# Starting the value sums with their first real products, and moving a row scaling from GpSimd to VectorE, in a transformer layer on one core

## The chip, the cores and the metric

The kernel runs on one core of one Trainium2 chip. The metric is device time of one execution in microseconds; lower is better. One program, written by hand for the five engines of the core, does the whole layer: TensorE multiplies, VectorE (DVE in the profile), ScalarE (ACT) and GpSimd (POOL) do elementwise work, and SyncE (SP) issues nearly all DMAs. Every engine takes its instructions strictly in the order in which the program lists them for it; one that has to wait holds those behind it.

## The reference

One layer over 2048 tokens of width 1024, with a context of 256 tokens, in float32. Cut to what matters here:

```
h  = modulate(rmsnorm(x), sh1, sc1)                 # and the same for the context
rq, rk, rv, rg, aq, ak, av = split(h @ w_in)
ret = gated bidirectional retention over rq, rk, rv  # 4 heads of 128, chunks of 128 tokens
q, k = rope(rmsnorm(aq)), rope(rmsnorm(ak))          # 8 heads of 64, 2 key/value heads
p   = softmax(q k^T / 8)                             # over 2304 keys (context and tokens)
att = p @ v
x  = x + g1 * (concat(ret, att) @ w_out)
h2 = modulate(rmsnorm(x), sh2, sc2)
x  = x + g2 * (relu(h2 @ w_ff1)^2 @ w_ff2)
out = rmsnorm(x)
```

The two places that the change touches are the sums `p @ v`, and the row scaling inside the second `rmsnorm(x)`, that of `h2`.

## The kernel before

**Precision.** Most products are made of parts: a float32 operand is split into a hi part (float16) and a lo part (what hi leaves out), and hi x hi, hi x lo and lo x hi are summed in PSUM.

**Stages.** The first stage (0 to about 690 us) computes the projections. The second (691 to about 1640) is attention, with the retention, the output projection and the second norm of finished token tiles woven in. The third (from about 1690) is the MLP. A scheduler orders the first stage; from attention on the order is written out by hand. There, work is entered with `on(k, phase, fn)` under a step number k and one of 13 phases; the steps run in order, and within each the phases: `begin, scores, piece, maximum, early, exp, cast, low, chain, pe, values, late, dma`. What is entered first in a phase of a step runs first. After the phases maximum, low and late, one link of a chain of small operations is also run (`link`); `settle(what)` runs links until the one wanted has been issued.

**Attention.** There are 32 groups (16 tiles of 128 queries, from the last tile to the first, times 2 key heads); a group has 18 steps, one for each tile of 128 keys. In every step TensorE makes the scores of one key tile (lines 202 and 203) and one piece of the products whose maximum the next group needs (line 165); VectorE reduces the piece (line 178); ScalarE takes the exponential (208) and, for two key tiles at once, the hi part (212); the lo part is made on GpSimd (219) for five of the nine pairs of key tiles and on VectorE (221) for the other four. `Group.values(j)` then multiplies the pair j: for each key tile and each of four heads, lo times the first 65 columns of the values, and hi times all 129 (values, a column of ones for the sum of p, and the values' lo part). Two heads share one PSUM bank, so a group has two banks `o`. Before the first pair, each bank is set by one product of a tile of zeros with 258 columns of values (`start=True`); everything after adds to it. Line 227 is that product, 235 and 236 are the lo and hi products. ScalarE evacuates the banks at the end of the group (240, 241).

**Output tiles.** For each token tile, `output_tile(t, k, last)` enters: the transposes of the retention half and of the attention half (line 1259, in steps k-11 and k-6), their hi parts on ScalarE and lo parts (`rl`, `al`) on VectorE (line 1266, steps k-9 and k-4), 16 x 3 products with w_out (1274 to 1276), the residual's additions on VectorE (1281), the squares' sums on ScalarE (1288), the store of the new x to DRAM on SP's queue (1291), and the chain for the root: a sum on VectorE (1295) and two operations on GpSimd (1009, and the power at 1010, `cy_f`). `made` is the step of the second addition; the store and the root are entered in step made+1, and `norm` in phase late of step made+4: it multiplies the whole tile `xr` (128 x 1024, in place) by the root, on GpSimd (1301). The transposes of the result (1306), their modulation on VectorE (1311) and GpSimd (1316) and their store follow some steps later. Tiles are 35 steps apart. For the last but one tile (t=1) made is step 619, so its norm is entered in step 623; for the last one (t=0) made is 642 and its norm is in step 646, and its transposes are taken up inside the MLP's first block.

**The start of the MLP.** The `prelude` (from step 606 on) enters loads and the forms of the first-layer weights (1451 on GpSimd, 1460 on ScalarE, 1461 on VectorE) and the first four of seven up products (1522 to 1524), whose sums are formed on VectorE (1545). After the last step the loop over the MLP's blocks begins; its first block holds up products 4 to 6 with their sums, the relu (1533, ScalarE), the squares (1534, GpSimd), the split of u (70, ScalarE; 71, VectorE), the split of the second-layer weights (70, 71), and then the down products (1582 to 1584) with the addition to the accumulator on VectorE (1585).

Of the kernel before, what the change touches and what calls it, by code (L numbers as in the profile page):

```python
# [13 lines left out]
F16 = mybir.dt.float16  # L14
# [3 lines left out]
ALU = mybir.AluOpType  # L18
# [4 lines left out]
P = 128  # L23
# [16 lines left out]
VW = 2 * HD + 1  # L40
# [14 lines left out]
def layer_kernel(ctx: ExitStack, tc: tile.TileContext, a: dict, out: bass.AP):  # L55
    nc = tc.nc
    mm = nc.tensor.matmul
# [76 lines left out]
    wv = kp.tile([P, 2, NK, VW + 1], F16, name="wv")  # L134
# [6 lines left out]
    class Group:  # L141
# [81 lines left out]
        def values(self, j):  # L223
            if j == 0:
                self.o = [psV.tile([P, 2, VW], F32, name=f"o{b}", tag=f"o{b}") for b in range(2)]
                for o in self.o:
                    mm(o, zeros, wv[:, 0, :2, :VW], start=True, stop=False)
            hi, lo = self.hi.pop(j), self.lo.pop(j)
            for i in range(2):
                v = wv[:, self.g, 2 * j + i]  # L230
                for h in range(4):
                    o = self.o[h // 2][:, h % 2]
                    c = slice(h * P, (h + 1) * P)
                    last = 2 * j + i == NK - 1 and h % 2 == 1
                    mm(o[:, : HD + 1], lo[:, i, c], v[:, : HD + 1], start=False, stop=False)  # L235
                    mm(o, hi[:, i, c], v[:, :VW], start=False, stop=last)  # L236

        def evacuate(self):
            self.so = op.tile([P, 4, VW], F32, name="so", tag="so")
# [20 lines left out]
    with ExitStack() as st:  # L260
# [630 lines left out]
        for n, (g, c) in enumerate(todo):  # L891
# [7 lines left out]
            last = c == len(PLAN[g]) - 1  # L899
# [49 lines left out]
    def pool(stack, name, bufs=1, **kw):  # L949
        return stack.enter_context(tc.tile_pool(name=name, bufs=bufs, reuse_waits="tile", **kw))  # L950
# [3 lines left out]
    vp = pool(attn, "vp")  # L954
# [12 lines left out]
    nc.vector.tensor_tensor(unit, ident[:, 64:65], ident[:, 96:97], op=ALU.add)  # L967
    nc.vector.tensor_tensor(unit, unit, ident[:, 80:81], op=ALU.add)
    nc.vector.tensor_scalar_mul(unit, unit, ROW)
    zeros = vp.tile([P, P], F16, name="zeros")  # L970
    nc.vector.memset(zeros, 0.0)
    mts = [vp.tile([P, 4, P], F32, name=f"mt{i}") for i in range(2)]
    for mt in mts:
        nc.gpsimd.memset(mt, 0.0)
# [27 lines left out]
    def settle(what):  # L1002
        while what not in settled:
            link()
# [243 lines left out]
    def output_tile(t, k, last):  # L1248
        y = {}
# [48 lines left out]

        def norm():
            settle(("f", t))  # L1300
            nc.gpsimd.tensor_scalar(y["x"], y["x"], y["r"], 1.0, op0=ALU.mult, op1=ALU.mult)

        def transpose_x(q):
            y["ps"] = bank(1)
# [33 lines left out]
        on(made + 1, "dma", store_x)  # L1338
        on(made + 1, "late", root)
        on(made + 4, "late", norm)  # L1340
        if last:
            for q in range(2):
# [53 lines left out]
    for n, t in enumerate(range(NT - 1, -1, -1)):  # L1396
        made_at, last = output_tile(t, R0 + 43 + RF * n, n == NT - 1)
# [410 lines left out]
```

## Time and profile before

| | |
|---|---|
| median of 3 runs | 2942.72 us (2941.49 to 2947.78) |
| the profiled execution | 2946.76 us |
| its span, first to last instruction | 2945.0 us |
| mean granted TensorE clock | 0.987 |
| HBM read, written | 272.52 MB, 71.46 MB |

| stretch, us | what runs | PE busy | DVE busy | ACT busy | POOL busy |
|---|---|---|---|---|---|
| 0 to 691 | projections | 629.05 | 476.70 | 233.07 | 287.58 |
| 691 to 1640 | attention and output tiles | 878.07 | 746.90 | 712.74 | 669.74 |
| 1640 to 1700 | last two output tiles, first MLP block | 49.07 | 33.90 | 21.92 | 34.58 |
| 1700 to 2945 | MLP | 1219.97 | 924.07 | 420.31 | 558.34 |

How to read it: times are in us of one profiled execution. A row of the profile names the line of the kernel, the engine, the operation, the tile written and those read, the shapes and the count. Matmuls are pipelined, so the 379 ns that a 128 x 512 product lasts overlap with the next one; the distance from one start to the next is what it takes of TensorE's time. PEld is the load of the weights, which runs beside the products. In rows of the timeline the first number is the start, the second the duration, and brackets hold the idle time of the engine before it with what ended it.

### The profile page before, as it was taken

The numbers are of one execution on the slowest core, as the hardware profiler recorded it, in microseconds if no ns is written. First come the engines' busy times: TensorE is split into PE (matmuls) and PEld (weight loads), VectorE is DVE, ScalarE is ACT, GpSimd is POOL, SyncE is SP. The second block draws the span as 40 slices with busy tenths as digits, with TensorE's granted clock in tenths as the row PEclk, the third lists the DMA queues.
The fourth block names the chain that finished last, engine by engine and source line by source line (L and its number), as shares of the span: only waits on it lengthen the run. The fifth ranks groups of instructions, "written<-read, shape, count | busy, mean of one in ns | idle before, by whom it ended". The sixth has DMA issues, their size and how long they took to land. (4 is left out here: it accounts for less than half of the span.)

```text
span 2945.0 us, 45295 instructions
## 1 busy us (share of the span) xinstructions
PE 2776.2 (94%) x17140; PEld 1648.8 (56%) x17140; DVE 2181.6 (74%) x3330; ACT 1388.0 (47%) x2280; POOL 1550.2 (53%) x1274
## 2 busy tenths in 40 slices
PE   7998898998799999999999899999999899999998
PEld 3777677775566666565666444444444344444443
DVE  5889847647987777777876577778777777777776
ACT  2333323325777777787777433333332333333332
POOL 3536326425876667887656656664443444444332
PEclk9999999999999999999999999999999999999999
DMA  9988843426412123332211723331114511111111
GB/s 300 340 283 280 271 154 107 160 67 201 137 46 81 49 63 121 90 104 85 73 63 51 273 92 101 104 102 60 53 51 154 173 60 47 54 51 51 58 44 58
DMA packets 265305, 346.95 MB, mean 118 GB/s; under 512 B 106231, under 2 KB 163831, under 8 KB 263294
## 3 DMA queue, kind: packets, MB, share of 16 engines
q1 hardware_dynamic: 254806, 336.57, 35.2%
q10 hardware_dynamic: 10280, 7.48, 0.9%
q8 instruction: 135, 2.21, 0.3%
q14 instruction: 84, 0.69, 0.1%
HBM read 272.52 MB, written 71.46 MB: 117 GB/s over the span
## 5 line engine op out<-in xcount | busy, mean ns | idle before, releaser
L178 DVE TENSOR_REDUCE nm<-mp 128x1 f32<-128x512 f32 (+1 forms) x576 | 390.9, 685 | 172.6 <-PE mp L165 143.3
L219 POOL TENSOR_TENSOR plo<-p,phi 128x1024 f16<-128x1024 f32 x160 | 353.7, 2212 | 172.9 <-ACT phi L212 139.6
L208 ACT ACTIVATE p<-st 128x512 f32<-128x512 f32 x576 | 338.1, 597 | 188.5 <-PE st L203 118.7
L1582 PE MATMUL pd<-w2hi,uhi 128*128 128x512 f16 x1024 | 388.0, 379 | 12.9 <-DVE acc L1585 12.6
L1583 PE MATMUL pd<-w2lo,uhi 128*128 128x512 f16 x1024 | 388.0, 379 | 0.6 <-DVE w2lo L71 0.6
L1584 PE MATMUL pd<-w2hi,ulo 128*128 128x512 f16 x1024 | 388.1, 379 | 0.0
L1585 DVE SCALAR_TENSOR_TENSOR acc<-pd,sc,acc 128x512 f32<-128x512 f32 x512 | 366.4, 739 | 5.7 <-PE pd L1584 5.6
L1522 PE MATMUL pu<-hf,w1f 128*128 128x512 f16 x896 | 340.1, 380 | 2.5 <-DVE q L1545 2.0
L1523 PE MATMUL pu<-hf,w1f 128*128 128x512 f16 x896 | 340.0, 379 | 0.0
L1524 PE MATMUL pu<-hf,w1f 128*128 128x512 f16 x896 | 339.8, 379 | 0.0
L824 PE MATMUL pso<-whi,hi_l 128*128 128x512 f32 (+1 forms) x768 | 295.8, 388 | 10.2 <-ACT xs L524 4.3
L212 ACT ACTIVATE phi<-p 128x1024 f16<-128x1024 f32 x288 | 303.8, 1055 | 0.0
L826 PE MATMUL pso<-whi,lo_l 128*128 128x512 f32 (+1 forms) x768 | 293.7, 383 | 4.1 <-DVE lo_l L67 4.1
L825 PE MATMUL pso<-wlo,hi_l 128*128 128x512 f32 (+1 forms) x768 | 292.9, 382 | 0.8 <-DVE wlo L67 0.7
L235 PE MATMUL o<-wv,plo 128*128 128x65 f16 x2304 | 235.9, 193 | 23.9 <-POOL plo L219 17.0
L221 DVE TENSOR_TENSOR plo<-p,phi 128x512 f16<-128x512 f32 x256 | 240.9, 942 | 18.6 <-ACT phi L212 15.7
L236 PE MATMUL o<-wv,phi 128*128 128x129 f16 x2304 | 243.8, 221 | 0.0
L235 PEld LDWEIGHTS <-plo 128*128 128x128 f16 x2304 | 206.7, 98 | 59.8 <-POOL plo L219 25.9
L202 PE MATMUL st<-qr,ks 128*128 128x512 f16 x576 | 220.2, 382 | 12.4 <-ACT p L208 10.4
L1534 POOL TENSOR_TENSOR r<-r 128x512 f32<-128x512 f32 x64 | 66.3, 1039 | 295.2 <-ACT r L1533 295.2
L203 PE MATMUL st<-qr,ks 128*128 128x512 f16 x576 | 220.0, 382 | 0.1
L165 PE MATMUL mp<-ks,qr 128*128 128x512 f16 x512 | 196.7, 384 | 23.0 <-DVE nm L178 22.2
(324 smaller groups left out, 5751.4 us busy)
## 6 DMA issues: line engine op xcount, KB each, us to landing
wm<-in_w_ff SPq DMA_DIRECT2D x64, 512.0 KB, 5.3
w1r<-in_w_ff SPq DMA_DIRECT2D x64, 512.0 KB, 4.6
ws<-in_w_ff SPq DMA_DIRECT2D x124, 256.0 KB, 3.5
wst<-in_w_in SPq DMA_DIRECT2D x60, 512.0 KB, 5.5
wst<-in_w_mod SPq DMA_DIRECT2D x32, 512.0 KB, 6.0
hf<-hp SPq DMA_DIRECT2D x56, 256.0 KB, 3.2
hf<-hf SPq DMA_DIRECT2D x14, 1024.0 KB, 7.1
orv<-rv SPq DMA_DIRECT2D x35, 256.0 KB, 4.0
```

The source lines that it names most:

```text
L178: nc.vector.tensor_reduce(dst, src, axis=AX.X, op=ALU.max, negate=True)
L208: nc.scalar.activation(self.p[kt // 2][:, kt % 2], self.s.pop(kt), AF.Exp, scale=HD**-0.5)
L212: nc.scalar.activation(hi, self.p[j], AF.Copy)
L219: nc.gpsimd.tensor_tensor(lo, p, hi, op=ALU.subtract)
L235: mm(o[:, : HD + 1], lo[:, i, c], v[:, : HD + 1], start=False, stop=False)
L1522: mm(pu[i], whi, hi, start=k == 0, stop=False)
L1523: mm(pu[i], whi, lo, start=False, stop=False)
L1524: mm(pu[i], wlo, hi, start=False, stop=k == 3)
L1582: mm(ps, uh, wh, start=f == 0, stop=False)
L1583: mm(ps, uh, wl, start=False, stop=False)
L1584: mm(ps, ul, wh, start=False, stop=f == NF - 1)
L1585: nc.vector.scalar_tensor_tensor(acc[:, c], ps, sc2, acc[:, c], op0=ALU.mult, op1=ALU.add)
```

## The change

The two products of zeros at the start of each group go, with the tile of zeros and its memset. In the first key tile of a group, the hi product of each head comes before its lo product, and for the first head of each bank it is the one with `start=True`. Everything else of `values` stays, its order in the other 17 key tiles too. And `norm` of `output_tile` runs on VectorE (`tensor_scalar_mul`) instead of GpSimd; its place in the order of the steps stays.

```diff
         def values(self, j):
             if j == 0:
                 self.o = [psV.tile([P, 2, VW], F32, name=f"o{b}", tag=f"o{b}") for b in range(2)]
-                for o in self.o:
-                    mm(o, zeros, wv[:, 0, :2, :VW], start=True, stop=False)
             hi, lo = self.hi.pop(j), self.lo.pop(j)
             for i in range(2):
                 v = wv[:, self.g, 2 * j + i]
@@
                     last = 2 * j + i == NK - 1 and h % 2 == 1
+                    first = j == i == 0
+
+                    if first:
+                        mm(o, hi[:, i, c], v[:, :VW], start=h % 2 == 0, stop=False)
                     mm(o[:, : HD + 1], lo[:, i, c], v[:, : HD + 1], start=False, stop=False)
-                    mm(o, hi[:, i, c], v[:, :VW], start=False, stop=last)
+                    if not first:
+                        mm(o, hi[:, i, c], v[:, :VW], start=False, stop=last)
@@
-    zeros = vp.tile([P, P], F16, name="zeros")
-    nc.vector.memset(zeros, 0.0)
@@
         def norm():
             settle(("f", t))
-            nc.gpsimd.tensor_scalar(y["x"], y["x"], y["r"], 1.0, op0=ALU.mult, op1=ALU.mult)
+            nc.vector.tensor_scalar_mul(y["x"], y["x"], y["r"])
```

## The prediction

> **What bounds the kernel now.** I read the page first, then busy time by stretches, then the rows of the two lines that go, then the timeline around the last two norms. The page gives the engines over the whole span:
>
> ```profile
> PE 2776.2 (94%) x17140; PEld 1648.8 (56%) x17140; DVE 2181.6 (74%) x3330; ACT 1388.0 (47%) x2280; POOL 1550.2 (53%) x1274
> ```
>
> TensorE is the engine to save time on, but only where nothing else ends last. The stretches (length, then busy PE, PEld, DVE, ACT, POOL, clock, DMA share, GB/s) tell where that is:
>
> ```profile
> 691.00:800.00 109.00, 88.31 (x875) 64.06 (x875) 100.37 (x194) 75.72 (x121) 81.52 (x56) 0.99 0.61 194
> 900.00:1100.00 200.00, 194.23 (x1815) 126.37 (x1813) 153.56 (x278) 155.32 (x255) 128.00 (x97) 1.00 0.19 59
> 1100.00:1350.00 250.00, 226.89 (x2080) 148.21 (x2078) 193.14 (x322) 188.68 (x313) 207.86 (x156) 0.99 0.36 105
> ...
> 1640.00:1700.00 60.00, 49.07 (x226) 22.70 (x225) 33.90 (x47) 21.92 (x42) 34.58 (x33) 0.97 0.81 303
> ```
>
> Attention runs from 691 to 1640. TensorE leads at 900 to 1100 (97%), and again after 1350; VectorE leads at first (100.37 of 109), GpSimd takes part from 1100 to 1350 (83%, TensorE 91%). From 1640 to 1700, where the last two token tiles are finished and the MLP begins, TensorE stands idle for 11 of 60 us and the DMA queues are nearly full. Both edits touch attention; the second also touches those 60 us.
>
> **The zero products.** Two of them go per group, 64 in all, with their weight loads:
>
> ```profile
> L227 PE MATMUL o<-wv,zeros x64: 272/274/274, 691.4 to 1615.8; 128*128 128x258 f16 x64
> ...
> 724.18 0.39 PE L227 MATMUL o<-wv,zeros 128*128 128x258 f16 x2
> 724.40 0.19 PE L235 MATMUL o<-wv,plo 128*128 128x65 f16 x1
> ```
>
> The 274 ns are a pipelined duration. What one costs is its slot: from 724.18 to 724.40 two slots passed, 0.11 us each, so 64 x 0.11 = 7.0 us. The products that take over their work existed already; each first hi product only moves ahead of its lo product and needs no operand that comes later, so no wait is added. The memset of the zeros (one on VectorE, 0.1 us at the start of the stage) is counted at nothing. Bounds: 0 (each slot turns into a wait for another engine) to -7.0. By stretches: four groups run before 800 with VectorE leading and gain nothing; some nine run between 1100 and 1350, taken at half; the other 19 count in full: (19 + 4.5) x 0.22 = 5.2. I take **-5.0**.
>
> **The norm, in attention.** Sixteen instructions leave GpSimd for VectorE; 13 meet VectorE while it still takes maxima, one falls in the last steps of attention, and two follow 1640.
>
> ```profile
> L1301 POOL TENSOR_SCALAR xr<-xr,cy_f x16: 1109/1120/2071, 873.6 to 1681.3; 128x1024 f32<-128x1024 f32 x16
> L416 DVE TENSOR_SCALAR x_l<-x_l,ry_x x16: 741/748/1230, 27.1 to 334.6; 128x1024 f32<-128x1024 f32 x16
> PEld bank L1306 <- POOL xr L1301: 4.8, 7, 1.3
> ```
>
> Line 416 is the same operation in the same shape on VectorE: 0.75 us alone, up to 1.23 beside GpSimd. GpSimd is busy around most norms, so I take 1.1, nearest to the 1.23. The third row (waits, 691 to 1640; us, times, longest) is what TensorE lost waiting for this norm: 4.8 us. On VectorE the norm comes sooner. One tile:
>
> ```profile
> 982.00 0.56 POOL L1010 TENSOR_TENSOR cy_f<-cv_f,half 128x1 f32<-128x1 f32 x1
> 987.56 1.67 POOL L1301 TENSOR_SCALAR xr<-xr,cy_f 128x1024 f32<-128x1024 f32 x1
> 984.99 0.69 DVE L178 TENSOR_REDUCE nm<-mp 128x1 f32<-128x512 f32 x1 [0.65 <-PE mp L165]
> 989.97 0.69 DVE L1311 TENSOR_TENSOR u<-bank,a 128x512 f32<-128x512 f32 x1 [0.54 <-PE bank L1306]
> ```
>
> The root is ready at 982.56, but the norm waits on GpSimd behind other work until 987.56. By program order it stands four maxima after the second residual addition, ahead of the maximum at 984.99: it would run from 984.3 to 985.4, partly in the 0.65 us that VectorE idled, and the 0.54 us before line 1311 disappears with the transposes' wait. What stands behind it on VectorE are maxima (TensorE waits for their banks) and low parts. Eight us from each of the 13 places show whether it is covered; three of the 13 rows and their sum:
>
> ```profile
> 874.00:882.00 8.00, 6.29 (x57) 4.41 (x58) 8.00 (x14) 6.18 (x10) 7.92 (x7) 1.00 0.00 0
> 984.00:992.00 8.00, 7.73 (x78) 5.51 (x75) 6.72 (x12) 6.05 (x12) 8.00 (x5) 1.00 0.07 25
> 1454.00:1462.00 8.00, 6.92 (x61) 4.91 (x62) 8.00 (x15) 6.19 (x9) 7.46 (x5) 1.00 0.08 29
> sum 104.00, PE 86.06 PEld 59.89 DVE 86.37 ACT 74.80 POOL 103.38; mean PE 6.62 PEld 4.61 DVE 6.64 ACT 5.75 POOL 7.95
> ```
>
> VectorE idles 17.6 of 104 us, but unevenly: in four stretches (874 and 1454, and two like them) it has 0 to 0.6 us, in the rest about 0.9 to 3.3. Four uncovered norms cost 4 x 1.1 = 4.4, and small waits for a late root or store 0.4; the 4.8 us of waits come back. Sum **0**. The Trainium skill (SBUF — State Buffer, section "Who interferes with whom") states that a VectorE operation of this kind takes a port pair which GpSimd shares, as an exclusive lock, and that whichever comes second waits out the other's whole instruction. By it the norm's price would be that of the slower rival below, +6.4 in this part in place of 0; the trace bears it out in part, since line 416 is lengthened to 1.23 but not by a whole instruction of GpSimd. Bounds: all 13 uncovered, +14.3 - 4.8 = +9.5; all covered, and the 1.1 us that GpSimd gains counted in the four tiles from 1100 to 1350 where it leads, -4.8 - 4.4 = -9.2.
>
> **The norm, in the last two tiles.** It works in place on the tile that the residual's store reads, so it must wait until that store has landed. GpSimd waited there with little behind it. VectorE has much behind it.
>
> ```profile
> 1650.49 0.32 SPq L1291 DMA_DIRECT2D x<-xr  x1
> 1653.06 0.56 POOL L1010 TENSOR_TENSOR cy_f<-cv_f,half 128x1 f32<-128x1 f32 x1
> 1657.36 1.12 POOL L1301 TENSOR_SCALAR xr<-xr,cy_f 128x1024 f32<-128x1024 f32 x1 [3.74 <-DMA x<-xr]
> 1652.83 0.69 DVE L1266 TENSOR_TENSOR rl<-bank,rh 128x512 f16<-128x512 f32 x1
> 1652.80 0.38 PE L1524 MATMUL pu<-hf,w1f 128*128 128x512 f16 x1
> 1653.58 0.66 PE L1259 MATMUL bank<-ident,ma 128*128 128x128 f32 x4 [0.40 <-DVE rl L1266]
> 1656.45 0.38 PE L1524 MATMUL pu<-hf,w1f 128*128 128x512 f16 x1
> 1658.53 0.66 PE L1306 MATMUL bank<-ident,xr 128*128 128x128 f32 x4 [1.70 <-POOL xr L1301]
> ```
>
> Tile 1's norm is issued in step 623, the last tile's low part (rl) in step 625, so VectorE would hold rl until the store lands: norm 1657.3 to 1658.1, rl to 1658.8. The transposes of the attention half (1653.58) need rl's bank, and TensorE is in order: it stands from 1653.0 to 1658.8, 5.8 us, where it had stood 0.6 + 1.9 = 2.4 us before 1653.58 and 1658.53. After that the norm's transposes are free to go at once. Net **+3.4**. SP's queue is not moved past: the store's issue (1650.49) stays.
>
> ```profile
> 1674.41 0.37 SPq L1291 DMA_DIRECT2D x<-xr  x1
> 1681.33 1.12 POOL L1301 TENSOR_SCALAR xr<-xr,cy_f 128x1024 f32<-128x1024 f32 x1 [5.06 <-DMA x<-xr]
> 1675.81 0.75 DVE L1461 SCALAR_TENSOR_TENSOR w1f<-w1r,sc,w1f 128x512 f16<-128x512 f32 x1 [0.45 <-ACT w1f L1460]
> 1676.47 0.68 DVE L1545 TENSOR_TENSOR r<-pu,w 128x512 f32<-128x512 f32 x1
> 1684.15 0.85 DVE L71 TENSOR_TENSOR ulo<-r,uhi 128x512 f16<-128x512 f32 x1 [1.92 <-ACT uhi L70]
> 1678.28 0.38 PE L1524 MATMUL pu<-hf,w1f 128*128 128x512 f16 x1
> 1682.51 1.12 PE L1306 MATMUL bank<-ident,xr 128*128 128x128 f32 x4 [3.85 <-POOL xr L1301]
> 1677.19 0.72 ACT L1533 ACTIVATE r<-r,scu 128x512 f32<-128x512 f32 x1 [1.42 <-DVE r L1545]
> 1677.82 0.61 ACT L70 ACTIVATE uhi<-r 128x512 f16<-128x512 f32 x1
> 1679.38 0.71 ACT L1460 ACTIVATE w1f<-w1s,sc 128x512 f16<-128x512 f32 x1
> 1689.19 1.11 DVE L71 TENSOR_TENSOR w2lo<-w2r,w2hi 128x512 f16<-128x512 f32 x1 [1.31 <-ACT w2hi L70]
> 1690.35 0.38 PE L1583 MATMUL pd<-w2lo,uhi 128*128 128x512 f16 x1 [0.61 <-DVE w2lo L71]
> 1682.00:1685.40 3.40, 2.90 (x9) 1.61 (x10) 1.48 (x3) 2.15 (x4) 2.45 (x3) 0.50 1.05 418
> ```
>
> The last tile's norm is issued in step 646, before the whole MLP loop. VectorE's eight operations from 1675.81 to 1682.2 (two first-weight forms, three sums of the up products, one u low part, two second-weight low parts) would start only after the norm, at 1681.9: 6.1 us late. Their order then runs like this. VectorE: form 0.75 and sum 0.68, to 1683.3. ScalarE, which stood behind that sum: relu 0.72, u high part 0.61, two second-weight high parts 0.57 each, the next form's high part 0.71, to 1686.4. VectorE, behind each of these: form's low part and the next sum, to 1687.75. ScalarE: relu and u high part, to 1689.1. So the second u low part starts at 1689.1 instead of 1684.15. From there VectorE does that low part, a weight's, a modulation, a form and the last sum (0.85 + 4 x 0.7, to 1692.6), ScalarE a relu and a weight's high part (to 1693.9), and the fourth second-weight low part starts at 1693.9 instead of 1689.19 and takes 1.1. TensorE gains 0.6 us at the transposes, then needs those two: its product at 1690.35 moves to 1695.0, **+4.6**. The sums and low parts behind it shift alike, so I take none of it as worked off. Each hold moves what follows, the second store too, so the two add.
>
> The clock: after TensorE's 3.85 us wait the granted clock was 0.50 for 3.4 us (last row), which at full half speed costs 1.7. The first hold, 5.8 us, is longer than that wait, so I add **+1.0** (bounds 0 and 1.7; the second hold already has its slow stretch, now hidden).
>
> Tail +3.4 + 4.6 + 1.0 = **+9.0**. Bounds: +3 (the first hold alone, the second worked off) to +13 (a landing 2 us later in each); a gain is excluded, since both rows of GpSimd show the store landing after VectorE reaches the place.
>
> Sum: -5.0 + 0 + 9.0 = **+4.0 us**. The profiled execution took 2946.76 us (span 2945.0), 0.14% above the median of 2942.72; on that scale 2950.8, on the median's **2946.7**.
>
> **The rivals.**
> Slower: in attention the norm waits out GpSimd's instruction. Line 416's 1.23 against 0.75 speaks for it, the 0.75 alone in most rows against it. At the 13 places GpSimd is busy 103.38 of 104 us, so a norm that has to wait out the instruction in progress there waits on average half of some 2.1 (its norms alone reach 2.07): 1.8 us instead of 1.1. That is 13 x 0.7 = 9.1 us more on VectorE; with 70% of it uncovered +6.4, sum +10.4, **2953**. It decides (past 0.2%, 5.9 us) once a norm in attention takes about 1.35 us. It is what the page named above would make of this move.
>
> Faster: TensorE bounds attention everywhere and VectorE's 17.6 idle us cover every norm: -7.0 - 4.8 = -11.8; and the second hold is worked off because GpSimd no longer delays the squares behind its own norm (its 5.06 us wait goes), leaving +3.4 + 1.0. Sum -7.4, **2935**. For it: TensorE's 97%; against it: the full stretches above.
>
> No hold: the norm meets a landed store in the tail. Sum -5.0, 2937.7, still no change; it has 0.05 of the chance. The 3.74 and 5.06 us of waiting for exactly this transfer speak against it.
>
> **How the numbers follow.** 0.2% or 5.9 us is about what this kernel's runs (2941.49 to 2947.78) can tell from no change. Forecast +4.0 with its own range -2 to +9 (terms +-2, +-3, +-4 together about 5): inside the bound 0.46 with the no-hold case; past it on the slow side 0.15 by a longer hold, and the slower rival 0.25: 0.40; faster rival 0.14. The range 2937 to 2954.5 takes in both rivals' near parts.
>
> **What would show it.** Line 227 absent and slots after its place closed up. No wait of TensorE for line 1301 in attention; line 1301 on VectorE at 0.75 to 1.25 us. VectorE idle for 3 to 4 us on the store before line 1266's rl, and 5 us before the MLP loop's first forms; TensorE idle about 5.8 us there, and 1640 to 1700 busy less than 49 of 60. Wrong it is if VectorE passes both norms without waiting, if attention shrinks by 10 us or grows, or if line 1301 averages 1.6 us.

## The result, and the profile after

The kernel after takes 2964.31 us (median of 4 runs, 2961.97 to 2965.47), the kernel before 2943.89 beside it (4 runs, 2941.49 to 2947.78): ratio 1.0067, 95% interval 1.005 to 1.0085. It is slower by about 20 us. The prediction was 2946.7 us with 2937 to 2954.5 as its range; the time lies outside it, on the slow side, past the slower rival's 2953 too. The profiled execution took 2963.85 us (span 2962.0, clock 0.987), 17 us more than that of before.

The stretches of the profile after, as those of before were read (length; busy PE, PEld, DVE, ACT, POOL; clock, DMA share, GB/s):

```profile
900.00:1100.00 200.00, 191.42 (x1783) 123.45 (x1782) 160.90 (x277) 154.11 (x253) 122.82 (x92) 1.00 0.19 59
1100.00:1350.00 250.00, 224.13 (x2071) 145.85 (x2070) 199.75 (x329) 189.05 (x315) 205.81 (x153) 0.99 0.35 105
691.00:1640.00 949.00, 861.42 (x8071) 568.72 (x8069) 766.09 (x1316) 708.12 (x1155) 652.29 (x474) 0.99 0.28 88
1640.00:1700.00 60.00, 48.90 (x254) 23.88 (x251) 23.73 (x41) 16.03 (x33) 25.90 (x28) 0.91 0.74 282
```

In attention (third row) VectorE is busy 19 us more than before (766.09 against 746.90) and TensorE 17 less (861.42 against 878.07): TensorE did less in the same time, about 7 us of it the slots of the zeros. In the 60 us of the last two tiles VectorE is busy 10 us less and the clock is 0.91 instead of 0.97.

Two rows of the timeline fence off the part of attention that holds every norm up to t=2: the evacuation of the second group and of the last. The third and fourth row are the last addition of tile 1 and of the last tile. Of before, then of after:

```profile
758.16 0.39 ACT L240 ACTIVATE so<-o 128x258 f32<-128x258 f32 x1
1638.65 0.39 ACT L240 ACTIVATE so<-o 128x258 f32<-128x258 f32 x1 [3.22 <-PE o L236]
1649.73 0.74 DVE L1281 SCALAR_TENSOR_TENSOR xr<-bank,sco,xr 128x512 f32<-128x512 f32 x1
1673.52 0.75 DVE L1281 SCALAR_TENSOR_TENSOR xr<-bank,sco,xr 128x512 f32<-128x512 f32 x1 [1.78 <-PE bank L1276]
```

```profile
756.16 0.39 ACT L243 ACTIVATE so<-o 128x258 f32<-128x258 f32 x1
1645.15 0.39 ACT L243 ACTIVATE so<-o 128x258 f32<-128x258 f32 x1 [3.21 <-PE o L239]
1655.77 0.74 DVE L1282 SCALAR_TENSOR_TENSOR xr<-bank,sco,xr 128x512 f32<-128x512 f32 x1
1685.41 0.75 DVE L1282 SCALAR_TENSOR_TENSOR xr<-bank,sco,xr 128x512 f32<-128x512 f32 x1 [1.84 <-PE bank L1277]
```

From the first of these rows to the second it is 880.49 us before and 888.99 after: **attention +8.5**. What comes after the second row is 10.5 us longer (span 2945.0 less 1638.65 against 2962.0 less 1645.15): **tail +10.5**. Ahead of the first row the two differ by 2.0 the other way. That offset arises ahead of the first norm, nearly all of it in the first stage, whose code is the same, and it differs from run to run (between -6.3 and +5.8 us in the kernels below). So each kernel below is also told by these two lengths, attention and tail, read from the same rows of its own trace as a difference to before.

The norm on VectorE by its line (durations are min/median/max in ns), and by its group (busy time, mean in ns, idle time before it):

```profile
L1302 DVE TENSOR_SCALAR xr<-xr,cy_f x16: 753/1621/2617, 872.1 to 1693.1; 128x1024 f32<-128x1024 f32 x16
```

```profile
L1302 DVE TENSOR_SCALAR xr<-xr,cy_f 128x1024 f32<-128x1024 f32 x16 | 25.5, 1594 | 13.5 <-DMA x<-xr 12.5 <-POOL cy_f L1011 0.9
```

The two of the tail take 0.753 each; 25.5 less those leaves 24.0 us for the 14 in attention, 1.71 each. Of the 12.5 us that it waited for the store 11.0 lie in the tail. In attention the first norm looks like this (timeline):

```profile
869.90 1.72 POOL L1108 TENSOR_TENSOR oqb<-oqt,tb 128x512 f32<-128x512 f32 x1
871.02 1.16 DVE L221 TENSOR_TENSOR plo<-p,phi 128x512 f16<-128x512 f32 x1
871.59 2.58 POOL L219 TENSOR_TENSOR plo<-p,phi 128x1024 f16<-128x1024 f32 x1
872.10 2.61 DVE L1302 TENSOR_SCALAR xr<-xr,cy_f 128x1024 f32<-128x1024 f32 x1
874.63 1.28 DVE L178 TENSOR_REDUCE nm<-mp 128x1 f32<-128x512 f32 x2
875.37 0.38 PE L165 MATMUL mp<-ks,qr 128*128 128x512 f16 x1 [2.17 <-DVE nm L178]
```

GpSimd's line 219 runs until 874.17, the norm until 874.71; the maxima behind it start then, and TensorE, which needs the banks that they free, stood 2.17 us. The waits of TensorE in attention (us, times, longest), before and then after:

```profile
PE mp L165 <- DVE nm L178: 20.6, 34, 2.0
PE bank L1306 <- POOL xr L1301: 3.5, 7, 1.1
PE mp L169 <- DVE nm L178: 1.4, 5, 0.6
```

```profile
PE mp L165 <- DVE nm L178: 32.0, 40, 2.3
PE mp L169 <- DVE nm L178: 5.9, 8, 2.2
```

The wait for the norm is gone (3.5 us), and the waits for maxima have grown by 11.4 and 4.5.

The tail, in the timeline of after:

```profile
1656.54 0.32 SPq L1292 DMA_DIRECT2D x<-xr  x1
1663.73 0.75 DVE L1302 TENSOR_SCALAR xr<-xr,cy_f 128x1024 f32<-128x1024 f32 x1 [5.00 <-DMA x<-xr]
1664.40 0.68 DVE L1267 TENSOR_TENSOR rl<-bank,rh 128x512 f16<-128x512 f32 x1
1665.14 1.11 PE L1260 MATMUL bank<-ident,ma 128*128 128x128 f32 x4 [5.47 <-DVE rl L1267]
1686.30 0.37 SPq L1292 DMA_DIRECT2D x<-xr  x1
1693.13 0.75 DVE L1302 TENSOR_SCALAR xr<-xr,cy_f 128x1024 f32<-128x1024 f32 x1 [5.98 <-DMA x<-xr]
1693.94 1.11 PE L1307 MATMUL bank<-ident,xr 128*128 128x128 f32 x4 [3.40 <-DVE xr L1302]
1701.88 0.38 PE L1583 MATMUL pd<-w2hi,uhi 128*128 128x512 f16 x1 [2.54 <-ACT w2hi L70]
1703.11 0.38 PE L1584 MATMUL pd<-w2lo,uhi 128*128 128x512 f16 x1 [0.85 <-DVE w2lo L71]
```

And three stretches of it, the granted clock third from the end:

```profile
1663.00:1669.90 6.90, 4.76 (x14) 2.25 (x15) 2.64 (x4) 0.60 (x1) 1.26 (x1) 0.51 0.77 286
1693.60:1697.00 3.40, 3.06 (x10) 1.62 (x11) 2.09 (x4) 1.82 (x4) 1.02 (x1) 0.51 1.05 418
1703.80:1710.80 7.00, 6.20 (x17) 2.42 (x18) 5.60 (x8) 3.51 (x6) 2.50 (x3) 0.51 0.24 71
```

Both holds are there as forecast: VectorE stands 5.00 and 5.98 us on the store, and TensorE 5.47 ahead of the attention half's transposes. Before, one stretch of 3.4 us ran at half clock; after, three did, 17 us together.

### The profile page after: what moved, and what is told of

The parts are those of the page before. It is cut to its first block, busy times and chain, and to the rows that moved or that the text cites. A ratio compares the mean times of both kernels' runs of the same rounds, so it can differ in the third digit from the quotient of the medians.

```text
span 2962.0 us, 45144 instructions
## 1 busy us (share of the span) xinstructions
PE 2770.6 (94%) x17076; PEld 1639.6 (55%) x17076; DVE 2206.5 (74%) x3345; ACT 1389.0 (47%) x2280; POOL 1534.2 (52%) x1258
## 5 line engine op out<-in xcount | busy, mean ns | idle before, releaser
L239 PE MATMUL o<-wv,phi 128*128 128x129 f16 x2176 | 233.3, 221 | 0.0
```

## The experiments

Theory A: on VectorE the norm is dear. In attention it is held until the instruction that GpSimd is in has ended, and delays the maxima that TensorE waits for; in the last two tiles it holds VectorE on the store. Theory B: the new start of the sums, with a hi product first, costs. The ratios compare each kernel with runs of before on the same chip (medians 2943.89 to 2947.17). Attention and tail (us, against the profiled run of before) are of one profiled execution each: kernels with the same attention as after read 8.8 and 9.7 beside its 8.5, and the six kernels with the tail of before read -1.3 to +2.5, on average +1.4. Part of this spread is TensorE's clock, which stands at half for stretches of 3.4 us that differ from trace to trace. Before has one at 1275.8, the kernel with the zeros tripled has none there, and in that group its offset to before falls by 1.6 us. In the tail before has one of 3.4 us, and five of those six have one of 6.8. So I take both lengths as good to about 2 us, and the tail of before as on the short side.

| kernel | median, us (runs) | ratio to before, 95% | attention | tail |
|---|---|---|---|---|
| after | 2964.31 (4) | 1.0067, 1.005 to 1.0085 | +8.5 | +10.5 |
| zeros only | 2945.74 (12) | 0.9993, 0.9982 to 1.0004 | -2.9 | +1.1 |
| norm only | 2970.03 (5) | 1.008, 1.0068 to 1.0093 | +13.0 | +10.5 |
| after, last two norms on GpSimd | 2958.82 (6) | 1.0043, 1.0029 to 1.0057 | +9.7 | +2.5 |
| after, only the last two on VectorE | 2956.48 (6) | 1.0038, 1.0024 to 1.0053 | -1.6 | +9.9 |
| before, 14 more reductions | 2954.25 (11) | 1.003, 1.0019 to 1.004 | +8.0 | +1.8 |
| before, 14 more scalings | 2955.07 (10) | 1.0033, 1.0022 to 1.0043 | +12.8 | -1.3 |
| diagonal matrix, no zeros | 2939.39 (11) | 0.9979, 0.9971 to 0.9988 | -1.0 | -2.8 |
| after, t=1's norm six steps later | 2958.73 (5) | 1.0045, 1.003 to 1.006 | +8.8 | +6.3 |
| diagonal matrix made on ScalarE, no zeros | 2943.4 (11) | 1.0001, 0.9992 to 1.001 | 0.0 | +1.8 |
| diagonal matrix, zeros kept | 2946.32 (11) | 1.0009, 1.0 to 1.0018 | +2.8 | -2.4 |
| before, zeros tripled | 2951.78 (10) | 1.0023, 1.0013 to 1.0032 | +5.5 | +2.3 |
| zeros gone, norm on ScalarE | 2946.18 (11) | 1.0003, 0.9994 to 1.0012 | -0.4 | +2.2 |

**The two parts apart.** The zeros alone (the edits in `values` and of the tile of zeros, `norm` as before), and the norm alone:

```diff
-            nc.gpsimd.tensor_scalar(y["x"], y["x"], y["r"], 1.0, op0=ALU.mult, op1=ALU.mult)
+            nc.vector.tensor_scalar_mul(y["x"], y["x"], y["r"])
```

> Only the value sums are changed; the norm stays on GpSimd. Theory A (the norm on VectorE is what costs: in attention it waits out the GpSimd instruction in progress, 1.7 us on average, and in the last two tiles it holds VectorE's queue until the store has landed; the zero products' slots come back in part): 3 to 6 us faster than before, 2938 to 2941. Theory B (the new beginning of the sums costs TensorE something itself, so that attention's growth is partly its doing): not faster, 2944 to 2952.

> Only the norm moves to VectorE; the zero products stay. Theory A: the whole change's +20 us and what the zeros gave, so +23 to +26, 2967 to 2970. Theory B: less than the whole change, +12 to +18, 2956 to 2962.

The zeros alone are within the noise of no change, on its fast side: theory A's 2938 to 2941 was missed, the median lies among theory B's 2944 to 2952, and the interval reaches from 5.3 us faster to 1.2 slower. The norm alone is 22.9 us slower than before by the medians, near theory A's +23 to +26 and above theory B's +12 to +18; with the zeros kept, nothing of that can be the new start. So theory B falls by the second kernel, and by the trace of the first: there the offset to before stays flat to the ninth group and then shrinks by 0.22 us in some groups only, 2.9 of the 7.0 us of slots, and grows by more than 0.02 nowhere.

In the trace of the norm alone the offset grows in jumps of up to 2.9 us at single tiles: 2.8 at the norm of 877.20, 2.9 at that of 1463.56, which last 2.62 us each. About 1 us of each jump is probably clock: right behind both norms, from 880.8 and from 1467.9, the granted clock is 0.50 for 3.4 us. In the kernel after, the norms of 872.10 and 1455.65 last as long, the clock behind them is 1.00, and the offset grows by 1.7 and 1.9.

**The norm's two places apart.** The whole change, with the norm on one engine or the other by tile:

```diff
-            nc.vector.tensor_scalar_mul(y["x"], y["x"], y["r"])
+            if t < 2:      # the other kernel: t >= 2
+                nc.gpsimd.tensor_scalar(y["x"], y["x"], y["r"], 1.0, op0=ALU.mult, op1=ALU.mult)
+            else:
+                nc.vector.tensor_scalar_mul(y["x"], y["x"], y["r"])
```

> The whole change, but the norm of the last two token tiles (t = 1 and 0) stays on GpSimd. Theory A: the holds on the store go, worth 10.6 us between the two traces: +9 to +11 against before, 2953 to 2955. A rival that the tail only takes over a delay from attention: no better than the whole change by more than 3 us, 2961 or more.

> The whole change, but only the last two token tiles have their norm on VectorE; the 14 in attention stay on GpSimd. Theory A: the tail's +10 less the zeros' 3 to 6: +4 to +7, 2948 to 2951. Theory B: +10 to +18, 2954 to 2962.

Both places cost, and each nearly alone: with the last two norms back on GpSimd the tail's 10.5 us fall to 2.5 and attention keeps its +9.7; with the others back, attention is -1.6 and the tail keeps +9.9. Both kernels are slower than theory A had them: +11.7 us by the medians in place of +9 to +11, and +9.3 (by the ratio +11.2, interval 7.1 to 15.6) in place of +4 to +7, where the zeros had been put in at 3 to 6. By its time alone the second lies in theory B's range (2954 to 2962); its attention of -1.6 speaks against theory B.

The three parts, each from a trace of its own, are the zeros (-1.6 to -2.9), the norm in attention (+13.0) and the tail (+10.5). They sum to 20.6 to 21.9, the trace of the whole change to 19.0 (8.5 and 10.5), and the medians differ by 20.4. Less the zeros, the three traces with the attention of after (8.5, 8.8 and 9.7) put the norm there at 10 to 13 us.

**What the time on VectorE costs, held and not held.** The norm stays on GpSimd; at its place, for t >= 2, VectorE gets one more instruction: a maximum over the whole tile, or a scaling by 1.0 in place.

```diff
         def norm():
             settle(("f", t))
+            if t >= 2:
+                y["e"] = sm.tile([P, 1], F32, name="ex", tag="ex")
+                nc.vector.tensor_reduce(y["e"], y["x"], axis=AX.X, op=ALU.max)
+                # the other kernel: nc.vector.tensor_scalar_mul(y["x"], y["x"], 1.0)
             nc.gpsimd.tensor_scalar(y["x"], y["x"], y["r"], 1.0, op0=ALU.mult, op1=ALU.mult)
```

> The kernel before, with 14 more instructions on VectorE: at the place of each norm of t>=2 a maximum over the whole tile xr (128 x 1024, one column out, not used), while the norm itself stays on GpSimd. It measures what a VectorE instruction of about this length costs at this place when it only takes time. Theory A (in attention the norm on VectorE is held until GpSimd's instruction in progress has ended, and this hold is what makes it dear): a reduction is not held; 14 of about 1.1 to 1.2 us each, no longer beside GpSimd, and the kernel some +6 to +10 us, less than with 14 extra scalings. Rival C (any instruction put ahead of the maxima costs its length, held or not): price in proportion to the length, about 0.55 us lost per us of VectorE, +9 us. Rival D (the price comes from the norm's wait for the root or for the store and not from VectorE's time): near 0, since this reduction waits for neither.

> As the run with 14 extra reductions, but the extra instruction is a scaling of xr by 1.0 in place on VectorE, the same form as the norm of the change; the norm itself stays on GpSimd. Alone it would take 0.75 us, less than the reduction. Theory A: it is held by GpSimd's instruction in progress, mean about 1.6 to 1.7 us, up to 2.6, and the kernel is +12 to +18 us, clearly above the reductions' price. Rival C: if it lasts 0.75 to 1.1 us, it costs no more than the reductions, +5 to +9. Rival D: near 0 where the store has landed; in place it also waits for the store.

The reductions, by their line and one of them in the timeline:

```profile
L1303 DVE TENSOR_REDUCE ex<-xr x14: 1203/1205/1222, 872.8 to 1624.5; 128x1 f32<-128x1024 f32 x14
```

```profile
985.08 2.14 POOL L219 TENSOR_TENSOR plo<-p,phi 128x1024 f16<-128x1024 f32 x1
985.68 1.22 DVE L1303 TENSOR_REDUCE ex<-xr 128x1 f32<-128x1024 f32 x1
```

The scalings, in the same two views:

```profile
L1302 DVE TENSOR_SCALAR xr<-xr x14: 679/1174/2078, 872.0 to 1628.0; 128x1024 f32<-128x1024 f32 x14
```

```profile
872.02 0.68 DVE L1302 TENSOR_SCALAR xr<-xr 128x1024 f32<-128x1024 f32 x1
982.68 2.14 POOL L219 TENSOR_TENSOR plo<-p,phi 128x1024 f16<-128x1024 f32 x1
983.29 2.08 DVE L1302 TENSOR_SCALAR xr<-xr 128x1024 f32<-128x1024 f32 x1
927.46 1.24 POOL L1010 TENSOR_TENSOR cy_f<-cv_f,half 128x1 f32<-128x1 f32 x1
927.98 0.68 DVE L1302 TENSOR_SCALAR xr<-xr 128x1024 f32<-128x1024 f32 x1
```

The hold is shown. All 14 reductions take 1.20 to 1.22 us, whatever GpSimd does beside them. The scaling that meets no work of GpSimd (872.02) takes 0.68; the one that starts 0.61 us into line 219 (983.29) ends at 985.37, 0.55 after that ends at 984.82, as the norm of after did (874.71 after 874.17). In the trace of after all 14 norms in attention end 0.55 us after an instruction of GpSimd. It works the other way too: the power of line 1010, 0.56 us at its shortest, takes 1.24 when a scaling starts beside it, and ends 0.04 after the scaling; a second one (1517.01) does the same. The Trainium skill (SBUF — State Buffer, section "Who interferes with whom") calls the shared port pair an exclusive lock; these durations agree with it. But by the recorded starts the power began 0.52 us before the scaling and yet ended behind it, so these rows don't show how it is decided who waits.

But the kernels' times did not part as theory A said. Theory A had the scalings at +12 to +18 us, clearly above the reductions. The scalings last 1.21 us on average instead of 1.6 to 1.7, since five of 14 meet no long instruction of GpSimd's and take 0.68, and both kernels spend 17 us on VectorE (16.9 and 17.0) and are 9 to 10 us slower. The two medians differ by 0.8 us, less than their intervals; the two traces by 4.8 in attention, and by 3.1 the other way in the tail. Whether a held us of VectorE costs more than a plain one stays open. Rival D (the price lies in the norm's waits for root or store) falls: the reductions wait for neither. What C said holds as to size: an instruction at this place costs about half to three quarters of its length (8.0 of 16.9; 12.8 of 17.0; the norm itself 13.0 of the 23.5 that it takes in that kernel), held or not. So what the hold is shown to do is to make the norm 1.71 us long instead of 0.75.

**A diagonal matrix.** Nobody scales the tile. GpSimd multiplies the identity by the roots, and the transposes become products with that matrix; nothing is written on the tile that the store reads.

```diff
-            nc.vector.tensor_scalar_mul(y["x"], y["x"], y["r"])
+            y["d"] = sm.tile([P, P], F32, name="dg", tag="dg", bufs=1)
+            nc.gpsimd.tensor_scalar(y["d"], ident, y["r"], 1.0, op0=ALU.mult, op1=ALU.mult)
...
-                nc.tensor.transpose(y["ps"][:, i], y["x"][:, (4 * q + i) * P : (4 * q + i + 1) * P], ident)
+                mm(y["ps"][:, i], y["x"][:, (4 * q + i) * P : (4 * q + i + 1) * P], y["d"], start=True, stop=True)
```

> The zeros are gone as in the change, and nobody scales the tile: GpSimd makes a diagonal matrix of the roots (128 x 128, one eighth of the norm's work), and the transposes of xr multiply by it in place of the identity. So nothing writes on the tile that the store reads, and the norm's wait for the store disappears in both of the last tiles, on either engine. Theory A: zeros -2 to -3, TensorE's waits for the norm in attention (4.8 us before) mostly gone, -2 to -4, the waits of 1.70 and 3.85 us in the last two tiles shortened by 1 to 4 us: 2934 to 2941, the fastest of all. Rival B (the start of the sums with the first hi product is itself dear): about the run with the zeros alone, 2945.

This is the fastest kernel of the study, faster than before and after, as theory A had it: ratio to before 0.9979 (0.9971 to 0.9988), 5.6 us. Its mechanism is shown in part only. Two further kernels took it apart: the matrix made on ScalarE (`nc.scalar.activation(y["d"], ident, AF.Copy, scale=y["r"])`), and the matrix with the zeros kept (the same two edits in the kernel before).

> As the run with the diagonal matrix (zeros gone, no norm), but the diagonal matrix is made on ScalarE instead of GpSimd, which frees 16 x 0.61 = 9.8 us of GpSimd. Theory A: from 1100 to 1350, where GpSimd takes part in setting the pace, 4 tiles x 0.6 = 2.4 us at most are won, and ScalarE, where the matrix (0.2 to 0.4 us) stands among exponentials, loses less: 2936 to 2940. Rival: ScalarE is late with exponentials and high parts, and it comes out 1 to 3 us slower than with GpSimd (2940 to 2943).

> The kernel before with the diagonal matrix alone; the zeros stay. If zeros and norm add up (theory A), it lies where the run with both lies, plus the 2 to 3 us that the zeros gave: ratio 0.9985 to 0.999, -3 to -4 us. Rival B (the zeros' going is worth nothing, what the run with both won is the diagonal's alone): ratio 0.998, -5 to -6 us.

Neither came out as either of its theories had it: the matrix alone is no faster than before (1.0009), and with ScalarE making it the gain is gone (1.0001). In the kernel with both, the groups of the transposes and of the matrix say what it costs:

```profile
L1308 PE MATMUL bank<-dg,xr 128*128 128x128 f32 x256 | 35.1, 280 | 2.0 <-DVE u L1313 0.6 <-POOL dg L1303 0.4
L1303 POOL TENSOR_SCALAR dg<-ident,cy_f 128x128 f32<-128x128 f32 x16 | 9.8, 610 | 0.2
```

A transpose by the identity was one pass (128 in all), a product with this other f32 matrix is two (256): 128 more slots of 0.11 us, 14 us of TensorE's time, which the expectation had not counted. That it eats up the waits saved (attention +2.8 with the zeros kept, -1.0 without) is likely, but no run shows it alone. By attention and tail together the kernel with both gains 3.8 us, by its median 5.6, and more than the sum of its parts (0.9993 and 1.0009). Why stays open; the tail's -2.8 is hardly more than the uncertainty given above, and its clock never falls to half there (1.00 from 1640 to 1700), where before has 3.4 us of it.

**The first hold alone.** The whole change, with t=1's norm behind rl and al of the last tile:

```diff
-        on(made + 4, "late", norm)
+        on(made + (10 if t == 1 else 4), "late", norm)
```

> The whole change, with the norm of the last but one tile entered six steps later, behind the low parts rl and al of the last tile on VectorE; the last tile's norm stays. Theory A: the first hold (TensorE idle 5.85 us ahead of the attention half's transposes, VectorE waiting 5.0 us for the store) vanishes and the window of granted clock 0.50 behind it too; about 4 us better than the whole change, 2958 to 2961. Rival B (the tail's loss comes from the last tile alone, and the first hold is made good behind it): no difference to the whole change, 2964.

The timeline, and a stretch:

```profile
1656.00 0.66 PE L1260 MATMUL bank<-ident,ma 128*128 128x128 f32 x4 [0.40 <-DVE rl L1267]
1660.31 0.75 DVE L1302 TENSOR_SCALAR xr<-xr,cy_f 128x1024 f32<-128x1024 f32 x1 [3.77 <-DMA x<-xr]
```

```profile
1657.00:1665.00 8.00, 5.53 (x30) 2.84 (x29) 2.04 (x3) 0.29 (x1) 1.74 (x2) 1.00 0.97 357
```

The transposes of the attention half wait 0.40 us instead of 5.47, the norm waits behind them, and the clock stays at 1.00. It is 5.6 us better than the whole change by the medians, as theory A had it, and 4.2 by the tail: the first hold's price, with the tail's 2 us of uncertainty (the intervals of the two ratios overlap). The other 6 us of the tail stay, with the last tile's norm where it was.

**What TensorE's time costs here.** The kernel before, with two more products of zeros for each bank:

```diff
                     mm(o, zeros, wv[:, 0, :2, :VW], start=True, stop=False)
+                    for _ in range(2):
+                        mm(o, zeros, wv[:, 0, :2, :VW], start=False, stop=False)
```

> The kernel before with two more products of zeros for each bank: 128 more slots of 0.11 us, 14.2 us of TensorE. It measures what TensorE's time costs at this place. If every slot counts (the prediction's upper bound, 7.0 for the 64 of the change): +14. At the share of the prediction's own value (5.0 of 7.0): +10. At the share that the run without zeros showed (2 to 3 of 7.0): +4 to +6, in the stretches 960 to 1100 and after 1320, and nothing before 960.

14.2 us of TensorE's time added cost 5.5 us by attention in the trace and 6.8 by the ratio, 0.39 to 0.48 of it. For the 64 slots that the change removed that is 2.7 to 3.4 of 7.0, as the zeros alone showed from the other side. The +4 to +6 of that share was a little low. The offset grows where it was expected to, by 2.2 us from 963 to 1106 and by 2.8 after 1322, but also by 1.3 before 963, and it falls by the 1.6 of the clock named above.

**The norm on the third engine.** Zeros gone, the 14 norms of attention on ScalarE, the last two on GpSimd:

```diff
+            if t >= 2:
+                nc.scalar.activation(y["x"], y["x"], AF.Copy, scale=y["r"])
+            else:
                 nc.gpsimd.tensor_scalar(y["x"], y["x"], y["r"], 1.0, op0=ALU.mult, op1=ALU.mult)
```

> The zeros are gone, and the 14 norms of t>=2 run on ScalarE instead of VectorE; those of t=1 and t=0 stay on GpSimd. Theory A (on VectorE it is dear because VectorE has little idle time in attention and the instruction is held by GpSimd's): on ScalarE nothing holds it, 14 of about 1.1 us each, and ScalarE is busy 0.75 of the time: within 3 us of the run with the zeros alone, 2943 to 2948. Rival C (any engine that does the norm at this place delays what TensorE waits for by about half of its length): ScalarE's exponentials and high parts are late, +6 to +9, 2951 to 2955.

Its line:

```profile
L1303 ACT ACTIVATE xr<-xr,cy_f x14: 1132/1148/1185, 876.7 to 1622.3; 128x1024 f32<-128x1024 f32 x14
```

Nothing holds it (1.13 to 1.19 us), and 16 us of ScalarE's time cost little: attention -0.4 against -1.6 and -2.9 with the norm on GpSimd, 1 to 2.5 us where VectorE lost 13. That is what theory A expected here (2943 to 2948). So it is not that any engine with the norm at this place delays TensorE by half its length: VectorE does.

## Why the prediction was wrong

By its steps:

- **The zeros, -5.0.** Mis-sized: -2.9 in the trace of that edit alone, 2.7 to 3.4 by the tripled zeros. The slots (0.11 us) were right; how many of the groups have TensorE as their limit was not. Nothing is gained up to the ninth group, where only the first four had been taken as nothing, and 13 groups (2.9 by 0.22) gave their slots, where 19 had been counted in full and nine at half. Busy 97% from 900 to 1100 did not mean that a slot saved is a slot won. In that edit's trace TensorE's waits grew instead (755 to 1640): for exponentials from 9.1 to 13.0 us, for maxima from 11.8 to 13.1.
- **The norm in attention, 0: the step that failed.** It was +13.0, or 10 to 13 with the whole change's traces, above its upper bound of +9.5. Two numbers in it were wrong. The duration, 1.1 us from the nearest row (line 416 with its maximum of 1.23), was 1.71: that row ran where GpSimd was busy 287.58 of 691 us, and the norm goes where GpSimd is busy 103.38 of 104, as the prediction had itself quoted. Its reading that line 416 was not lengthened by a wait for GpSimd's instruction was wrong too. The row at 332.17 started 0.51 us into GpSimd's instruction and ended 0.56 after its end. A nearer row, in attention itself, stood in the same trace of before (rows below): line 221, 0.67 us at its shortest, is lengthened in 101 of its 256 instructions, up to 2.63 us, and all of these end some 0.55 us after an instruction of GpSimd. And the cover: four of 13 norms were taken as uncovered because VectorE idled 0.9 to 3.3 us in the other eight-us stretches. But about half to three quarters of VectorE's added time was lost, in every kernel that added some. My reading, which no run shows by itself, is that its idle time in a stretch is spread in waits for TensorE, and that a maximum delayed now makes TensorE late with the bank that the next maximum waits for. The waits for the norm that were booked as won back (4.8 us) did go, and waits for maxima grew by more (11.4 and 4.5).
- **The slower rival** had the mechanism and the duration (1.8 us, measured 1.71), and the prediction named the mark that would decide it, 1.35 us. It stayed too small (+6.4 in this part) because it added the longer duration alone and kept the cover. It had a chance of 0.25 in place of the greater one.
- **The last two tiles, +9.0.** Right: +10.5, within 3 to 13, by the two holds that were named (+9.1 against the mean tail of the six kernels that left it alone). From tile 1's last addition to the last tile's the offset to before grew from 6.0 to 11.9, by 5.9 us (forecast 3.4 + 1.0), and moving that norm away won 4.2 to 5.6; from there to the end it grew by 5.1 (forecast 4.6). The clock was worse than its term: two more stretches at half speed instead of one, and longer ones (6.9 and 7.0 us). Half of TensorE's busy time in those two (4.76 and 6.20) is 5.5 us, my estimate of the most that they cost, against the 1.0 put in. If they cost nearly that, the holds themselves cost less than the 8.0 put in, and that the sum came out so close is partly luck. One of its figures does not follow from its rows either: TensorE's waits before 1653.58 and 1658.53 are 0.40 and 1.70 there, 2.1 us and not 2.4.
- **No hold, and faster:** neither came. VectorE stood 11.0 us on the two stores.
- **What would show it:** of the marks for being wrong, two came, attention growing and line 1301's average (now line 1302) at 1.6 us.

The rows of before at lines 416 and 221, each with what GpSimd did beside it:

```profile
331.66 1.18 POOL L493 TENSOR_TENSOR t<-xs,rtb 128x256 f32<-128x256 f32 x1
332.17 1.23 DVE L416 TENSOR_SCALAR x_l<-x_l,ry_x 128x1024 f32<-128x1024 f32 x1
L221 DVE TENSOR_TENSOR plo<-p,phi x256: 673/689/2635, 691.8 to 1635.1; 128x512 f16<-128x512 f32 x128
851.29 2.13 POOL L219 TENSOR_TENSOR plo<-p,phi 128x1024 f16<-128x1024 f32 x1 [0.35 <-ACT phi L212]
851.33 2.63 DVE L221 TENSOR_TENSOR plo<-p,phi 128x512 f16<-128x512 f32 x1
```

Put together, the parts make -3 + 13 + 10.5 = 20.5 against 20.4 by the medians and 19.0 by the trace of the whole change; that the first two agree so well is chance, since each part is good to about 2 us. By these parts, of the miss of 17.6 us some 13 lie in the norm's step, 2 in the zeros, 1.5 in the tail, and 1.2 in the median of before, 2943.89 beside this kernel instead of 2942.72.

## What to carry to other kernels

Before moving an elementwise operation between VectorE and GpSimd, look at what GpSimd runs at the new place, not at the operation's mean in another stage: for a scaling like this one, where GpSimd is never idle, take the rest of its instruction in progress plus about 0.55 us as the duration, and look for a row at that place that is already lengthened so. An engine's idle share is no safe cover: in this attention loop time added on VectorE, which hands back the banks, cost about half of its length or more, time saved or added on TensorE, the busiest, less than half, and time added on ScalarE a tenth or so. These shares are of this kernel; elsewhere they have to be measured. And an operation that works in place on a tile that is being stored belongs on an engine with nothing behind it, or behind the work that others wait for.

## What the runs showed of the hardware

- A held scaling ends 0.54 to 0.56 us after GpSimd's instruction (all 14 norms in attention in the kernel after), though alone it takes 0.68 to 0.75: the hold does not add the whole duration.
- The low part on VectorE (line 221), with two inputs and 0.67 us at its shortest, shows the same: started at 871.02 beside line 1108 it ended at 872.18, 0.56 after that one's end at 871.62.
- In attention and the tail TensorE's clock stands at half in stretches of about 3.4 us or twice that, and their length does not follow from the wait alone: 3.4 us at TensorE's wait of 3.85 before, 6.8 at a wait of 3.89 with the zeros alone, 6.9 at one of 5.47 after. The Trainium skill (TensorE: Matmul & The Clock Gate, Part 1) gives the window in which activity is judged as 3413 ns; one such window of half speed, and two, agree with that.
- A transpose of an f32 tile by the identity is one pass, its product with the f32 diagonal matrix of the same shape two (128 and 256 instructions, 0.28 us each, one every 0.11).
